# The order of the expert blocks in a two-layer mixture-of-experts trunk: pairs spread evenly, blocks with further rows in every other round

## The chip, the cores and the metric

The kernel runs on one core of one Trainium2 chip. The metric is the device time of one execution in microseconds (us), the median of several runs. TensorE (PE) does the matmuls, VectorE (DVE) and ScalarE (ACT) work element by element, GpSimd (POOL) gathers and scatters rows by index, SyncE (SP) issues the loads of weights from HBM.

## The reference

A trunk of two layers on 1024 frames of 1024 features in fp32. Each layer is a mixer followed by a hierarchical mixture of experts; only the latter is touched:

```python
MOE_EXPERTS = 32; MOE_TOPK = 2; MOE_HIDDEN = 512      # 4 groups of 8 experts
def expert_block(args):
    xb, e = args
    return (jax.nn.silu(xb @ w_gate[e]) * (xb @ w_up[e])) @ w_down[e]
...
out = jnp.zeros((n_tok + 1, d), ys.dtype).at[row_tok].add(ys * row_gate[:, None].astype(ys.dtype))
```

Each frame goes to two of the 32 experts. An expert has gate and up matrices of 1024 x 512 and a down matrix of 512 x 1024, 6 MB in all, so one layer reads 192 MB of expert weights. The order in which experts are worked off doesn't change the result.

## The kernel before

The expert stage of a layer is the function `moe` (L757 to L1016). The experts are ranked by how many frames chose them, and three kinds of blocks follow from the rank:

- a **large block** (`expert`, L861) for each of the 16 experts with most frames (NBIG): 128 rows. Its matmuls are done as three products of split numbers: each half tile of weights is split by ScalarE into whi (L138) and by VectorE into the rest wlo (L139), the rows likewise into xh and xl, and PE adds whi xh, wlo xh and whi xl (`three`, L841);
- the first four of these (NEXT) carry **further rows** too, up to 64 more: they are multiplied with the raw weight tile (L877, L903), which stays occupied until then;
- a **pair** (`pair`, L910) for two of the 16 smaller experts, 64 rows each, side by side in the PE array, with raw weights in fp32 (L919, L928). It needs both experts' weights, 12 tiles of 1 MB, a large block 6.

Inside every block the steps are: a gather of the rows (L790), eight transposes of them (`turn`, into ps_t), gate and up (into ps_g and ps_u), hs = silu(gate) (ACT, L848) times up (DVE, L849), four transposes of hs (into ps_h, L106, called **the turn** below), for a large block its split into hh and hl, down (into ps_y), the evacuation y (DVE, L858) and a scatter (L796). From the last matmul of up to the first of down PE depends on DVE, ACT and its own turn in sequence: **the joint**.

Weight tiles come through a ring: 10 tiles in layer 0, 6 in layer 1. SP issues the loads in the order of the blocks, each when its tile of the ring is free: a large block's tile is free when it is split (or, with further rows, when their matmuls are done), a pair's when PE has read it. The split halves have 7 buffers each for whi and wlo.

The order of the blocks is the list `plan` (L948 to L952): four times a large block with further rows and a pair, then four times three plain large blocks and a pair. The last blocks of the list also decide what `route_over` (L976, the bookkeeping for frames beyond the blocks' rows) stands beside: it is written after the ninth block. Within each engine the instructions stand in a fixed order that a scheduler makes ahead of time from the program; it puts instructions of neighbouring blocks between each other. At run time no engine changes its order.

Of the kernel before, what the change touches and what calls it, by code (L numbers as in the profile page):

```python
# [26 lines left out]
NBIG = 16  # L27
NEXT = 4
# [8 lines left out]
class Core:  # L37
# [725 lines left out]
    def moe(self, o, ctx):  # L763
# [183 lines left out]

        plan, big = [], 0  # L948
        for q in range(NPAIR):
            n = 1 if q < NEXT else 3  # L950
            plan += [("big", b) for b in range(big, big + n)] + [("pair", q)]
            big += n  # L952
        rows = []
        for what, b in plan:
            c = b if what == "big" else NBIG + b
# [1239 lines left out]
```

## Time and profile before

| | |
|---|---|
| median of 3 runs | 3067.4 us (3063.31 to 3076.72) |
| the profiled execution: time, span | 3067.31 us, 3065.6 us |
| mean granted TensorE clock over the span | 0.897 |
| busy over the span: PE, DVE, ACT, POOL | 87%, 58%, 37%, 27% |
| expert stage of layer 0, first to last block | about 824 to 1415 us |
| expert stage of layer 1 | about 2412 to 3005 us |

Busy time of PE is the time with a matmul under way; idle time in a stretch is its length less the busy time. DMA share is the mean busy share of the 16 DMA engines. A wait names the instruction that waited and what released it. In the timeline equal neighbours are merged (x8 means eight), and "idle before" is the engine's own idle time ahead of the row.

### The profile page before, as it was taken

What the parts mean: (1) busy time and instruction counts of PE and PEld (TensorE: products, weight loads), DVE (VectorE), ACT (ScalarE), POOL (GpSimd) and SP (SyncE); (2) the same over time, 40 slices, a digit from 0 to 9 for tenths busy, and PEclk for the clock granted to TensorE, in tenths of its full rate; (3) what the DMA queues carried; (4) which work ended last, traced back from release to release, by engine and by line L of the source; (5) the groups of instructions that cost most, each with busy time, mean ns of one, the idle gap of its engine ahead of it and who ended that gap; (6) DMA issues with size and microseconds to landing.
All of it is one profiled execution on the core that took longest, in us unless ns stands there. A gap on an engine that the chain in (4) does not pass through costs nothing. (4 is left out here: it accounts for less than half of the span.)

```text
span 3065.6 us, 39902 instructions
## 1 busy us (share of the span) xinstructions
PE 2658.0 (87%) x14357; PEld 1855.2 (61%) x14357; DVE 1790.3 (58%) x3207; ACT 1125.4 (37%) x1781; POOL 834.4 (27%) x1161
## 2 busy tenths in 40 slices
PE   4987788989699999995899999999978799998991
PEld 4776456647454466662677777777876444566660
DVE  7546999655633467764734555646557434556674
ACT  4311455432222245552433323323233223345451
POOL 5250665224211031101302533354015111121102
PEclk8898699989799999997898977886988799999996
DMA  8747220223588899997645322243333689999996
GB/s 279 177 125 203 58 59 19 86 69 103 214 336 343 348 368 407 377 388 252 262 132 179 106 73 79 74 115 102 103 124 124 235 343 367 367 363 403 382 385 250
DMA packets 344954, 672.82 MB, mean 219 GB/s; under 512 B 118527, under 2 KB 259871, under 8 KB 293040
## 3 DMA queue, kind: packets, MB, share of 16 engines
q1 hardware_dynamic: 272896, 611.23, 54.5%
q10 hardware_dynamic: 56752, 25.41, 3.1%
q0 software_dynamic: 15104, 33.58, 3.0%
q8 instruction: 115, 1.88, 0.3%
q14 instruction: 87, 0.71, 0.1%
HBM read 611.31 MB, written 79.79 MB: 225 GB/s over the span
## 5 line engine op out<-in xcount | busy, mean ns | idle before, releaser
L139 DVE TENSOR_TENSOR wlo<-w,whi 128x1024 fp32r<-128x1024 f32 x384 | 451.1, 1218 | 112.9 <-ACT whi L138 111.4
L138 ACT ACTIVATE whi<-w 128x1024 fp32r<-128x1024 f32 x384 | 390.3, 1054 | 235.9 <-PE ps_g L841 70.5
L240 PE MATMUL ps_b<-hTh,wh 128*128 128x512 f32 x608 | 260.4, 430 | 26.6 <-ACT cc L1388 12.4
L241 PE MATMUL ps_b<-hTl,wh 128*128 128x512 f32 x608 | 257.0, 423 | 0.0
L790 POOL DMA_INDIRECT xg<-h_d,tok x56 | 80.9, 1445 | 639.6 <-PE ps_t L106 613.1
L242 PE MATMUL ps_b<-hTh,wl 128*128 128x512 f32 x608 | 254.9, 419 | 0.0
L849 DVE TENSOR_TENSOR hs<-hs,ps_u 128x512 f32<-128x512 f32 x48 | 32.9, 685 | 263.3 <-PE ps_u L919 212.4
L796 POOL DMA_INDIRECT ye_d<-y,tab x48 | 71.4, 1487 | 422.3 <-DVE y L858 329.4
L167 DVE SCALAR_TENSOR_TENSOR adacc<-w,cs,adacc 128x256 f32<-128x256 f32 x329 | 162.5, 511 | 5.2
L139 DVE TENSOR_TENSOR wl<-w,wh 128x1024 fp32r<-128x1024 f32 x84 | 104.2, 1255 | 100.8 <-ACT wh L138 100.8
L240 PEld LDWEIGHTS ps_b<-hTh,wh 128*128 128x128 f32 x608 | 125.2, 207 | 54.7 <-ACT cc L1388 13.2
L313 DVE TENSOR_TENSOR_SCAN sP<-keep,sP,sbz 128x256 f32<-128x256 f32 (+1 forms) x160 | 134.8, 885 | 22.7 <-ACT keep L300 10.7
L848 ACT ACTIVATE hs<-ps_g 128x512 f32<-128x512 f32 x48 | 28.7, 598 | 325.0 <-PE ps_g L919 244.7
L919 PE MATMUL ps_g<-w,xh 128*64 128x512 f32 x512 | 143.5, 598 | 0.0
L138 ACT ACTIVATE wh<-w 128x1024 fp32r<-128x1024 f32 x84 | 86.3, 1053 | 154.1 <-PE ps_b L241 135.3
L242 PEld LDWEIGHTS ps_b<-hTh,wl 128*128 128x128 f32 x608 | 124.8, 205 | 28.7 <-issue 0.4
L241 PEld LDWEIGHTS ps_b<-hTl,wh 128*128 128x128 f32 x608 | 125.2, 206 | 27.4 <-issue 0.4
L133 POOL TENSOR_TENSOR rs<-rm,nhalf 128x1 f32<-128x1 f32 (+2 forms) x56 | 48.5, 867 | 330.3 <-DVE rm L131 294.3
L919 PE MATMUL ps_u<-w,xh 128*64 128x512 f32 x512 | 137.6, 595 | 0.0
L315 POOL TENSOR_TENSOR sw<-sw,sP 128x512 f32<-128x512 f32 (+1 forms) x80 | 99.2, 1241 | 135.3 <-DVE sP L313 61.9
L928 PE MATMUL ps_y<-w,hh 128*64 128x512 f32 x512 | 122.0, 598 | 2.2 <-ACT hh L923 2.2
L1705 POOL TENSOR_TENSOR T<-N,X 128x60 f32<-128x60 f32 (+24 forms) x248 | 85.8, 346 | 126.5 <-DMA N<-n_d 108.3
(712 smaller groups left out, 6178.9 us busy)
## 6 DMA issues: line engine op xcount, KB each, us to landing
w<-in_moe_w_gate_dram SPq DMA_DIRECT2D x128, 1024.0 KB, 14.6
w<-in_moe_w_up_dram SPq DMA_DIRECT2D x128, 1024.0 KB, 14.6
w<-in_moe_w_down_dram SPq DMA_DIRECT2D x128, 1024.0 KB, 13.4
w<-in_ada_w_dram SPq DMA_DIRECT2D x48, 1024.0 KB, 6.0
w<-in_odd_w_in_dram SPq DMA_DIRECT2D x26, 1024.0 KB, 5.6
cy<-ye_d SPq DMA_DIRECT2D x16, 1024.0 KB, 14.5
cx<-xm_d SPq DMA_DIRECT2D x21, 512.0 KB, 7.2
w<-in_even_w_in_dram SPq DMA_DIRECT2D x8, 1024.0 KB, 8.6
```

What stands on the lines that cost most here:

```text
L138: self.nc.scalar.activation(hi, x, AF.Copy)
L139: self.nc.vector.tensor_tensor(lo, x, hi.bitcast(FT), op=OP.subtract)
L167: eng.scalar_tensor_tensor(acc, wk, ck, acc, op0=OP.mult, op1=OP.add)
L240: nc.tensor.matmul(p, a[0], b[0], start=first, stop=False)
L241: nc.tensor.matmul(p, a[0], b[1], start=False, stop=False)
L242: nc.tensor.matmul(p, a[1], b[0], start=False, stop=last)
L313: v.tensor_tensor_scan(P[:, r, 0:n][:, ::-1], keep[:, r, 0:n][:, ::-1], zero.to_broadcast([128, n]), P[:, r, n:n + 1], op0=OP.mult, op1=OP ...
L315: g.tensor_tensor(w[:, :, 0:n], w[:, :, 0:n], P[:, :, 1:n + 1], op=OP.mult)
L790: nc.gpsimd.indirect_dma_start(out=xg, out_offset=None, in_=h_d[:], in_offset=bass.IndirectOffsetOnAxis(ap=tokc, axis=0), bounds_check=T - ...
L919: nc.tensor.matmul(ps[z][r], x[:, 4 * h + k, r], w[z][h][:, k, :], start=(h == 0 and k == 0), stop=(h == 1 and k == 3))
L928: nc.tensor.matmul(py[n][r], ht[:, f, r], w[2][f // 2][:, f % 2, two[n]], start=(f == 0), stop=(f == 3))
L1705: g.tensor_tensor(o, N[:, 0:j, j:j + 1].to_broadcast([128, j, w]), X[:, j:j + 1, c:8].to_broadcast([128, j, w]), op=OP.mult)
```

## The change

```diff
--- before.py
+++ after.py
@@ -947,9 +947,9 @@
 
         plan, big = [], 0
         for q in range(NPAIR):
-            n = 1 if q < NEXT else 3
-            plan += [("big", b) for b in range(big, big + n)] + [("pair", q)]
-            big += n
+            n = q // 2 if q % 2 == 0 else NEXT + big
+            big += q % 2
+            plan += [("big", n), ("pair", q), ("big", NBIG - 1 - q)]
         rows = []
         for what, b in plan:
             c = b if what == "big" else NBIG + b
```

NPAIR is 8, NBIG 16, NEXT 4. Before, the plan is, with the number of each large block: 0, pair, 1, pair, 2, pair, 3, pair, 4, 5, 6, pair, 7, 8, 9, pair, 10, 11, 12, pair, 13, 14, 15, pair. After: 0, pair, 15, 4, pair, 14, 1, pair, 13, 5, pair, 12, 2, pair, 11, 6, pair, 10, 3, pair, 9, 7, pair, 8: eight rounds of a large block, a pair and a plain large block. Blocks 0 to 3, those with further rows, open the first, third, fifth and seventh round. The same blocks run, with the same weights; the order of gathers, loads and scatters follows the plan, and so does the scheduler's order on every engine.

On PE, layer 0, the joint of the tenth large block of the plan before (the last plain one before a pair). ps_u, ps_g and ps_y are written by gate, up and down; L919 is the pair that follows:

```order
L841 MATMUL ps_u<-whi,xl 128x512
L106 MATMUL ps_h<-ident,hs 128x128 x4
L919 MATMUL ps_g<-w,xh 64x512
L106 MATMUL ps_t<-ident,xg_6647 128x128 x8
L919 MATMUL ps_g<-w,xh 64x512 x7
L919 MATMUL ps_u<-w,xh 64x512 x8
L919 MATMUL ps_g<-w,xh 64x512 x8
L841 MATMUL ps_y<-whi,hh 128x512
L841 MATMUL ps_y<-wlo,hh 128x512
L841 MATMUL ps_y<-whi,hl 128x512
```

After, PE, layer 0, the joint of the plain large block that closes the fourth round (number 12):

```order
L841 MATMUL ps_u<-whi,xl 128x512
L106 MATMUL ps_t<-ident,xg_6643 128x128 x8
L106 MATMUL ps_h<-ident,hs 128x128 x4
L841 MATMUL ps_y<-whi,hh 128x512
L841 MATMUL ps_y<-wlo,hh 128x512
L841 MATMUL ps_y<-whi,hh 128x512
L841 MATMUL ps_y<-wlo,hh 128x512
L841 MATMUL ps_y<-whi,hl 128x512 x2
```

Before, 24 matmuls of the pair stand between the turn and down; after, down follows the turn directly, and only the next block's transposes stand ahead of the turn.

On DVE, layer 0, from hs of the sixth pair of the plan before; the first two evacuations y are those of the large block ahead of it, the other two its own; xl and wlo are splits of rows and weights of what follows:

```order
L849 TENSOR_TENSOR hs<-hs,ps_u 128x512
L139 TENSOR_TENSOR xl<-ps_t,xh 128x512 x2
L139 TENSOR_TENSOR wlo<-w,whi 128x1024 x3
L858 TENSOR_TENSOR y<-ps_y,g2row 128x512 x2
L139 TENSOR_TENSOR wlo<-w,whi 128x1024 x8
L858 TENSOR_TENSOR y<-ps_y,g2row 128x512 x2
L139 TENSOR_TENSOR wlo<-w,whi 128x1024
L849 TENSOR_TENSOR hs<-hs,ps_u 128x512
L139 TENSOR_TENSOR wlo<-w,whi 128x1024 x2
L139 TENSOR_TENSOR xl<-ps_t,xh 128x512 x2
```

After, from hs of the sixth round's pair; again the first two evacuations are those of the large block ahead of it and the last two its own:

```order
L849 TENSOR_TENSOR hs<-hs,ps_u 128x512
L139 TENSOR_TENSOR xl<-ps_t,xh 128x512 x2
L858 TENSOR_TENSOR y<-ps_y,g2row 128x512 x2
L139 TENSOR_TENSOR wlo<-w,whi 128x1024 x9
L825 COPY xh<-ps_t 128x512
L139 TENSOR_TENSOR wlo<-w,whi 128x1024
L849 TENSOR_TENSOR hs<-hs,ps_u 128x512
L139 TENSOR_TENSOR wlo<-w,whi 128x1024 x2
L139 TENSOR_TENSOR hl<-ps_h,hh 128x512
L858 TENSOR_TENSOR y<-ps_y,g2row 128x512 x2
```

Before, the pair's evacuations stand ahead of the next large block's hs; after, they stand behind that block's hl.

## Rows read from the trace of the kernel before

**Rows 1.** Stretches of the expert stages: busy us and (x) instructions by engine, clock, DMA
```profile
core 0: us, PE busy (x) PEld busy (x) DVE busy (x) ACT busy (x) POOL busy (x), PEclk, DMA share, GB/s
824.00:1072.70 248.70, 243.56 (x1051) 120.12 (x1051) 90.90 (x136) 70.71 (x89) 25.37 (x24) 1.00 0.85 340
1072.70:1415.00 342.30, 323.06 (x1426) 213.59 (x1425) 221.81 (x239) 170.88 (x196) 55.69 (x28) 1.00 0.92 372
2412.60:2660.60 248.00, 244.02 (x1047) 121.77 (x1045) 90.55 (x132) 74.28 (x93) 26.58 (x25) 0.99 0.84 337
2660.60:3005.00 344.40, 324.20 (x1432) 214.35 (x1431) 221.90 (x242) 167.69 (x193) 46.78 (x27) 1.00 0.96 384
2930.10:3005.00 74.90, 72.87 (x319) 46.53 (x317) 42.02 (x45) 32.38 (x37) 4.64 (x4) 1.00 0.98 404
```

**Rows 2.** What PE waited for, 1072.7 to 1415 us: total, times, longest
```profile
PE ps_h L106 <- DVE hs L849: 8.5, 9, 1.6
...
PE ps_g L841 <- DVE wlo L139: 3.1, 4, 1.2
...
PE ps_g L841 <- ACT whi L138: 2.4, 3, 1.6
...
PE ps_u L841 <- DVE wlo L139: 0.9, 2, 0.7
```

**Rows 3.** The same of 2660.6 to 3005 us
```profile
PE ps_h L106 <- DVE hs L849: 8.7, 7, 2.5
...
PE ps_y L841 <- DVE y L858: 2.7, 1, 2.7
...
PE ps_g L841 <- DVE wlo L139: 1.8, 3, 0.8
...
PE ps_g L841 <- ACT whi L138: 1.6, 2, 1.2
...
PE ps_u L841 <- DVE wlo L139: 0.3, 1, 0.3
```

**Rows 4.** Timeline of PE: start, us, instruction, in brackets idle before and releaser
```profile
1088.09 1.04 PE L106 MATMUL ps_h<-ident,hs 128*128 128x128 f32 x4 [1.60 <-DVE hs L849]
...
1108.50 1.23 PE L106 MATMUL ps_t<-ident,xg 128*128 128x128 f32 x8 [0.46 <-ACT xh L823]
...
1111.84 0.49 PE L841 MATMUL ps_g<-whi,xh 128*128 128x512 f32 x1 [1.63 <-ACT whi L138]
...
1175.99 0.75 PE L106 MATMUL ps_h<-ident,hs 128*128 128x128 f32 x4 [0.85 <-DVE hs L849]
...
1407.63 2.80 PE L928 MATMUL ps_y<-w,hh 128*64 128x512 f32 x12 [0.69 <-ACT hh L923]
...
2676.63 0.74 PE L106 MATMUL ps_h<-ident,hs 128*128 128x128 f32 x4 [2.50 <-DVE hs L849]
...
2680.87 0.50 PE L841 MATMUL ps_y<-whi,hl 128*128 128x512 f32 x1 [1.07 <-DVE hl L139]
...
2764.23 0.74 PE L106 MATMUL ps_h<-ident,hs 128*128 128x128 f32 x4 [1.84 <-DVE hs L849]
...
2768.98 0.47 PE L841 MATMUL ps_y<-whi,hh 128*128 128x512 f32 x1 [2.75 <-DVE y L858]
2769.29 0.39 PE L841 MATMUL ps_y<-wlo,hh 128*128 128x512 f32 x1
2769.52 0.40 PE L841 MATMUL ps_y<-whi,hl 128*128 128x512 f32 x1
```

**Rows 5.** What the load queue (SP) waited for, 824 to 1072.7, then 1072.7 to 1415
```profile
SPq L943 <- PE ps_e L903: 61.6, 8, 17.6
...
SPq L943 <- PE ps_e L877: 54.4, 10, 14.9
...
SPq L943 <- DVE wlo L139: 111.5, 49, 6.4
```

**Rows 6.** Timeline of PE: the last pair of layer 1, its down matmuls
```profile
2999.68 4.89 PE L928 MATMUL ps_y<-w,hh 128*64 128x512 f32 x22
```

## The prediction

> **What bounds the kernel now.** I read the page's 40 slices first: between 800 and 1420 us and between 2410 and 3010 us, the expert stages of the two layers, TensorE (PE), the DMA share and the TensorE clock are all near their tops at once. The diff touches these two stages alone, some 1190 of 3065.6 us. Then I cut each stage where the order of blocks changes: a first stretch in which large blocks with further rows and pairs alternate (four of each), and a second with three plain large blocks to each pair (twelve and four). In the first, PE is busy 243.56 of 248.70 us and 244.02 of 248.00, with a DMA share of 0.85 and 0.84; in the second 323.06 of 342.30 and 324.20 of 344.40, with 0.92 and 0.96 [rows 1]. So the first stretch is PE's: its idle time is 5.1 and 4.0 us, 1.8%. The second is nearly DMA's as well, and PE idles 19.2 and 20.2 us there, 5.7%. The clock is granted in full, 0.99 to 1.00. Nothing that PE does is removed by the change: before and after, each layer has the same matmuls on it. **The gain therefore has a hard end**: if every idle microsecond of both stages went, 5.1 + 4.0 + 19.2 + 20.2 = 48.5 us would be won.
>
> What is that idle time? The waits of PE in the second stretch name it. The transposes of the hidden rows (L106 into ps_h) wait for the product hs: 8.5 and 8.7 us. The matmuls that wait for split weights (whi, wlo), so for weights that came late, make 3.1 + 2.4 + 0.9 = 6.4 us in layer 0 and 1.8 + 1.6 + 0.3 = 3.7 us in layer 1 [rows 2, 3]. The first kind isn't supply: it is the joint inside a large block, where gate and up are done, ScalarE and VectorE form hs, PE turns it, both engines split it, and only then down can start. PE is in order, so a joint costs what the order puts into it. A joint with seven matmuls of the next large block inside idles 0.85 us. A bare one, with no expert matmul between the turn and down, idles 1.60 us; 2.50 + 1.07 = 3.57; 1.84 + 2.75 = 4.59; and, with the next block's eight transposes ahead of the turn, 0.46 + 1.63 = 2.09 [rows 4].
>
> **The change, part by part.** The sum starts at the profiled execution, 3067.31 us (its span of 3065.6 and 1.7 around it), beside the median of 3067.4.
>
> Supply. Before, the second stretch asks for 30 weight tiles per 85.6 us (342.3 over four groups) and the first for 18 per 62.2 us (248.7 over 4). After, every round of large block, pair, plain block asks for 24. Rounds with further rows are longer on PE than on DMA, so the loads, which in the first stretch wait for tiles that the further rows hold (61.6 + 54.4 us, against 111.5 us for splits in the second) [rows 5], get time to run ahead; plain rounds eat that lead. I count all 10.1 us of late weights as gone, less the 1.63 that I price in the joints: **-8.5 us**. Its ends are 0 and -10.1.
>
> Joints. The program orders each engine ahead of time, and this is what the diff doesn't show. I counted for the 24 plain large blocks of both layers whether at most one expert matmul stands between the turn and down. Before, 4 are bare (the four above): 1 with the transposes ahead of the turn, 3 without. After, 20 are: 12 with, 8 without; blocks that overlapped now stand one behind the other. That adds 11 of the one kind and 5 of the other. A bare joint costs more than a filled one by 2.09 - 0.85 = 1.24 us in the first kind, and by the mean of 1.60, 3.57 and 4.59, 3.25, less 0.85 = 2.40 in the second [rows 4]: 11 x 1.24 + 5 x 2.40 = **+25.6 us**. Nothing covers it: PE is the engine whose end sets the stage. For the low end the 12 lose only the 0.46 of the transposes and the 0.69 that a pair waits for its hh [rows 4], 0.30 over a filled joint, and the 5 lose 1.60 - 0.85 = 0.75: 3.3 + 3.8 = 7 us. For the high end all 16 cost 4.59 - 0.85 = 3.74: 60 us. I take the middle because the rows are of the same two kinds; the low end has a point in its favour, since after, down often begins with the four matmuls that read hh before the first that reads hl.
>
> VectorE's order. In layer 0's sixth round the pair's evacuations now stand behind hl of the plain block that follows, whose down matmuls need the pair's two banks; before, the sixth pair's stood ahead of the next block's hs. The 2.75 us wait for an evacuation in layer 1 [rows 3, 4] is such a case, and one of the four bare joints. Not counted again.
>
> The rest. The further rows' matmuls are the same and are cut into as many pieces within a handful: 0. The bookkeeping of the overflow (L976) still falls beside a block with further rows and the plain one behind it: 0. The order of the mixer between the two stages shifts a little too, with the same instructions: 0, and 6 us either way, a guess. The stage ends on a plain block instead of a pair: its bare joint is counted.
>
> Sum: 3067.3 - 8.5 + 25.6 = **3084 us**, 0.55% slower. About 0.5% (15 us) is what a measurement of this kernel can tell from no change.
>
> **Rivals.** (A) *Faster, 3040 us.* The change evens out the demand, and PE idles everywhere as it does in the first stretch, 1.8%. Then the second stretches' 39.4 us of idle time become 686.7 x 0.018 = 12.6, and 26.8 us are won. For it: the two stretches have different scarce resources [rows 1]. Against it: most of the idle time named in rows 2 and 3 is joints, and the order after makes them bare; it decides once a bare joint costs no more than a filled one. The Trainium skill, page "Perfetto Trace Analysis", section "Optimization Strategy", says that where the most-contended engine changes between regimes, interleaving the regimes may help. By that rule the outcome is this rival. The trace agrees that there are two regimes (DMA share 0.85 against 0.92, 0.84 against 0.96), but it also shows the second with PE busy at 94%, so that little is left to mix. The same page of the Trainium skill, section "Identifying the Most-Contended Engine", warns that matmul busy time is no measure of headroom; here the starts 0.23 us apart in a full run [rows 4] are what I rest on, and the pace that stands in them can't be changed by an order.
>
> (B) *No difference, 3066 us.* Supply as above and joints at their low end: 3067.3 - 8.5 + 7. For it: the four hh matmuls ahead, and idle times that overlap with late weights. It is also what comes out if both resources are so full that any order gives the same pace.
>
> (C) *Slower still, 3106 us.* The plain rounds run out of weights. A pair's PE time is 96 x 4.89/22 = 21.3 us [rows 6] and 2.1 of transposes; a plain large block's is then (323.06 - 4 x 23.4)/12 = 19.1. A plain round needs 2 x 19.1 + 23.4 + joints of some 6 = 68 us of PE. Its 24 tiles of 1.05 MB and its gathers and scatters, about 3 MB, take 28.3/0.384 = 74 us at the second stretch's rate in layer 1 [rows 1]. It is 6 us short unless the round before ran ahead, and the ring of weight tiles is 6 deep in layer 1 (10 in layer 0). If the lead fails in layer 1, four rounds lose 22 us; in both layers 44, 3128. Against it: the rate reached 404 GB/s in the last group [rows 1], and rounds with further rows have some 10 us to spare.
>
> **How the numbers follow.** Forecast 0.40, A 0.12, B 0.34, C 0.14. The range leaves out A and the upper half of C, and takes in B with the mixer's 6 us and late weights at their end: 3058 to 3112. Faster by over 0.5% is A, 0.12. The same is B, 0.34. Slower is the forecast and C, 0.54.
>
> **What would show it.** Right: PE's idle time within each expert stage rises from 24 us to some 33; its waits for hs, hh and hl grow, and those for whi and wlo shrink; the DMA share is even at about 0.9. A: idle time falls to 15 us a stage. B: it stays at 24, with other names. C: waits for whi and wlo grow in the plain rounds, and with them a DMA share near 1 there. I am wrong at the root if the busy time itself changes, by the clock or by matmuls that run at another pace, or if the difference lies outside the two stages.

## The result

The changed kernel takes 3133.91 us (median of 4 runs, 3130.29 to 3154.07) beside 3069.68 for the kernel before (4 runs, 3063.31 to 3076.72): 1.0229 times as long, 95% interval 1.0209 to 1.025. It is slower, as forecast, but by 64 us and not by 17, and 3133.91 lies above the range (3058 to 3112).

Where the 64 us lie is read by cutting both traces into the first expert stage, the mixer between the stages, and the second expert stage. First the kernel before, then the changed one; the columns are those of [rows 1].

```profile
core 0: us, PE busy (x) PEld busy (x) DVE busy (x) ACT busy (x) POOL busy (x), PEclk, DMA share, GB/s
823.70:1415.10 591.40, 566.92 (x2476) 334.01 (x2475) 313.11 (x374) 241.71 (x285) 81.05 (x52) 1.00 0.89 359
1415.10:2412.70 997.60, 862.69 (x5859) 690.61 (x5859) 549.41 (x1126) 330.89 (x660) 319.42 (x605) 0.83 0.42 131
2412.70:3005.00 592.30, 568.13 (x2476) 336.09 (x2475) 312.40 (x374) 241.96 (x285) 73.37 (x52) 0.99 0.91 365
```

```profile
821.80:1437.40 615.60, 582.16 (x2476) 335.50 (x2475) 312.76 (x374) 241.03 (x285) 75.68 (x52) 0.98 0.86 344
1437.40:2448.20 1010.80, 863.63 (x5858) 690.15 (x5858) 542.97 (x1125) 330.67 (x660) 310.01 (x605) 0.83 0.42 129
2448.20:3069.30 621.10, 586.73 (x2477) 343.86 (x2475) 313.20 (x374) 240.20 (x285) 76.93 (x52) 0.97 0.87 348
```

The stages grew by 24.2 and 28.8 us, the mixer by 13.2, and what comes before is 1.9 shorter: 64.3. In each stage, take busy from length: PE's idle time went from 24.5 to 33.4 us and from 24.2 to 34.4, together +19.2. **But its busy time rose as well**, by 15.2 and 18.6 us, with the same matmuls. The DMA share fell. The mixer has nearly the same busy time as before (862.69, 863.63); 12 of its 13 us are idle time.

What PE waited for in the changed kernel, layer 0 and then layer 1 (total us, times, longest); [rows 2, 3] answer to them for the second stretches:

```profile
PE ps_h L106 <- DVE hs L849: 11.7, 12, 2.0
PE ps_y L841 <- ACT hh L138: 4.7, 9, 0.7
PE ps_y L841 <- DVE hl L139: 4.1, 6, 1.2
PE ps_y L841 <- DVE y L858: 3.9, 2, 2.8
PE ps_g L841 <- DVE wlo L139: 2.8, 4, 1.5
...
PE ps_u L841 <- DVE wlo L139: 1.0, 1, 1.0
```

```profile
PE ps_h L106 <- DVE hs L849: 11.9, 13, 1.8
PE ps_g L841 <- DVE wlo L139: 5.3, 6, 1.5
PE ps_y L841 <- ACT hh L138: 3.4, 6, 0.7
PE ps_y L841 <- DVE y L858: 3.2, 2, 2.1
...
PE ps_y L841 <- DVE hl L139: 2.3, 6, 1.0
...
PE ps_g L841 <- ACT whi L138: 1.4, 2, 1.2
```

The joint's waits (hs, hh, hl and y, a pair's 0.7 for hh in each layer with them) make 25.1 and 21.5 us, where the same rows of the kernel before make 11.0 and 13.9: +21.7. Late weights (whi, wlo) make 3.8 and 6.7 us instead of 7.7 and 5.0: -2.2. So the added idle time is the joints', as the prediction said. The kernel before, its whole stage of layer 0:

```profile
PE ps_h L106 <- DVE hs L849: 9.6, 11, 1.6
PE ps_g L841 <- DVE wlo L139: 4.4, 6, 1.2
...
PE ps_g L841 <- ACT whi L138: 2.4, 3, 1.6
```

One bare joint in TensorE's timeline of the changed kernel, with the next block's transposes ahead of the turn:

```profile
1277.77 1.23 PE L106 MATMUL ps_t<-ident,xg 128*128 128x128 f32 x8 [0.46 <-ACT xh L823]
1279.76 0.75 PE L106 MATMUL ps_h<-ident,hs 128*128 128x128 f32 x4 [0.76 <-DVE hs L849]
1283.32 0.47 PE L841 MATMUL ps_y<-whi,hh 128*128 128x512 f32 x1 [2.81 <-DVE y L858]
...
1283.86 0.43 PE L841 MATMUL ps_y<-whi,hl 128*128 128x512 f32 x1
1284.10 0.62 PE L841 MATMUL ps_y<-whi,hh 128*128 128x512 f32 x1
1284.52 0.63 PE L841 MATMUL ps_y<-wlo,hh 128*128 128x512 f32 x1
```

```profile
1278.00:1284.00 6.00, 2.43 (x15) 1.99 (x15) 6.00 (x8) 5.05 (x6) 2.15 (x2) 1.00 1.01 421
1284.00:1287.50 3.50, 3.50 (x10) 2.67 (x9) 3.18 (x3) 0.00 (x0) 0.00 (x0) 0.51 1.03 421
```

Idle 0.46, 0.76 and 2.81 us, with VectorE busy throughout (6.00 of 6.00). And **then the clock falls**: the granted clock is 1.00 up to 1284 and 0.51 behind it, which is the 1.2 GHz level, and the matmuls start 0.42 us apart instead of 0.23. By the trace's record of the clock, it stood at that level for 22.0 and 33.9 us of the two stages, in the kernel before for 5.2 and 10.3. At half pace, half of these 40.4 us more would be lost, 20 us. The starts of all matmuls in the two traces give the split of the 33.8 us by which busy time rose, each matmul counted up to the start of the next and compared with the mean of its line in unbroken runs at the full clock, in the kernel before: 21.8 us are in matmuls at the lower level, 6.6 in those just ahead of and just behind a gap, 4.6 where one kind of matmul follows another, 0.8 in all others. At the edge of a gap a matmul adds more because in a run it shows 0.39 us of busy time and adds 0.23, while the last one before a gap adds all of it and the first behind adds 0.31.

The Trainium skill, page "TensorE: Matmul & The Clock Gate", section "Part 1: The HAM clock gate (the "warmup" mystery)", says that the array is at its lower clock by default and that activity releases it. The rows above agree: the clock falls behind 6 us of which PE was busy for 2.43. The last section shows a fall that busy time alone does not explain.

### The profile page after: what moved, and what is told of

Read it like the earlier page. It is cut to its first block, busy times and chain, and to the rows that moved or that the text cites. A ratio compares the mean times of both kernels' runs of the same rounds, so it can differ in the third digit from the quotient of the medians.

```text
span 3129.6 us, 39865 instructions
## 1 busy us (share of the span) xinstructions
PE 2689.2 (86%) x14357; PEld 1860.8 (59%) x14357; DVE 1783.7 (57%) x3207; ACT 1122.5 (36%) x1781; POOL 827.0 (26%) x1161
## 5 line engine op out<-in xcount | busy, mean ns | idle before, releaser
L919 PE MATMUL ps_u<-w,xh 128*64 128x512 f32 x512 | 140.6, 595 | 0.0
L241 PEld LDWEIGHTS ps_b<-hTl,wh 128*128 128x128 f32 x608 | 122.9, 202 | 27.8 <-issue 0.8
L919 PE MATMUL ps_g<-w,xh 128*64 128x512 f32 x512 | 139.0, 597 | 0.0
L928 PE MATMUL ps_y<-w,hh 128*64 128x512 f32 x512 | 137.5, 613 | 1.4 <-ACT hh L923 1.4
L841 PE MATMUL ps_y<-whi,hh 128*128 128x512 f32 x256 | 107.5, 422 | 15.2 <-ACT hh L138 8.1
```

What stands on the lines that cost most here:

```text
L241: nc.tensor.matmul(p, a[0], b[1], start=False, stop=False)
L841: nc.tensor.matmul(p, x[a][:, k, :], w(b, j)[:, ns], start=(first and a + b == 0), stop=(last and a == 1))
L919: nc.tensor.matmul(ps[z][r], x[:, 4 * h + k, r], w[z][h][:, k, :], start=(h == 0 and k == 0), stop=(h == 1 and k == 3))
L928: nc.tensor.matmul(py[n][r], ht[:, f, r], w[2][f // 2][:, f % 2, two[n]], start=(f == 0), stop=(f == 3))
```

## Experiments

In them J is the theory of the prediction, with the clock added: bare joints cost idle time, and the clock falls in them. S is rival C: weights come late in the new order. H came up on the way: blocks with further rows hold their weight tiles too long, so the loads stop. "Bare" counts all joints with at most one expert matmul between the turn and down, now of pairs and of blocks with further rows too (these have a second turn; the last one counts): **10 and 9 before, 22 and 16 after**, in layers 0 and 1.

### One layer at a time (l0new, l1new)

```diff
+        if i == 0:
             plan, big = [], 0
             for q in range(NPAIR):
                 n = q // 2 if q % 2 == 0 else NEXT + big
...
+        else:
+            plan, big = [], 0
+            for q in range(NPAIR):
+                n = 1 if q < NEXT else 3
...
```

(l1new has `if i == 1`.)

> The new order of blocks in layer 0 only; layer 1 keeps the old one. The rows of the changed kernel lay 24.2 us in layer 0's expert stage, 13.3 us in the mixer behind it, 28.6 us in layer 1's expert stage. Theory J (bare joints on TensorE's queue, idle time and a clock that falls in them): the pieces add, since each stage carries its own bare joints. Layer 0's stage about 615 us (before 591.3), layer 1's about 592 as before; the mixer, whose instructions stand on TensorE in exactly the order of the changed kernel here, about 1011 (before 997.6). Time 3105 us, ratio 1.0115. Theory S (supply: weights that come late in rounds without further rows, worst in layer 1, whose ring of tiles is the smaller): layer 0 gives less than half, under 1.010. If the mixer's 13 us were chance and not its order: ratio about 1.007.

> The new order of blocks in layer 1 only. The mixer stands on TensorE in exactly the order of the kernel before. Theory J: layer 0's stage 591, mixer 998, layer 1's stage about 621 (before 592.4): time 3098 us, ratio 1.0093. If the mixer's 13 us came from anything but its order, the mixer is near 1011 here. Theory S: layer 1 is the place where weights run out, ratio over 1.010 and the waits for split weights (whi, wlo) over 15 us, against 6.7 in the changed kernel.

Measured: l0new 1.0154 (1.0123 to 1.0184), l1new 1.0096 (1.0074 to 1.0117). The first stage and the mixer of l0new, then the mixer and the second stage of l1new; their other stages took 592.7 and 595.2 us:

```profile
823.80:1439.50 615.70, 582.34 (x2476) 335.36 (x2475) 312.95 (x374) 240.83 (x285) 72.50 (x52) 0.98 0.86 344
1439.50:2456.40 1016.90, 872.76 (x5858) 697.50 (x5858) 546.17 (x1126) 330.79 (x660) 311.40 (x605) 0.82 0.42 129
```

```profile
1423.10:2423.50 1000.40, 859.43 (x5859) 688.21 (x5859) 549.19 (x1126) 330.71 (x660) 318.29 (x605) 0.83 0.43 131
2423.50:3036.30 612.80, 579.04 (x2476) 337.03 (x2475) 312.81 (x374) 240.45 (x285) 76.53 (x52) 0.99 0.87 352
```

The pieces add (1.54% and 0.96% beside 2.29%), and each stage is slow only where its blocks are new. S fails in both: l0new is over its 1.010, l1new under it, with 5.2 us of waits for weights where S asked for over 15. J's 1.0115 for l0new is missed by a mixer of 1017 us. **The mixer's loss goes with the mixer's own order**: 1011 and 1017 us in the two kernels that have the new one, 998 and 1000 where it is the old one (and 995 and 996 in before_pin2 and before_ring, which have the old one too). Its size isn't firm, though: after_hi and after_hi_pin2 below have one order there on every engine and mixers of 1011 and 1027 us, at a granted clock of 0.83 and 0.81. Layer 1 came out 8 us better than in the changed kernel with PE in the same order: the clock was at its lower level for 12.8 us here and for 33.9 there, and PE was busy 7.7 us less. So 8 of that stage's 29 us are not fixed by the order.

### Joints filled by hand (after_pin, before_pin, after_pin2, before_pin2)

```diff
-                expert(xg, ws[0], ...)
+                g = expert(xg, ws[0], ...)
...
+            m = next(g)
+            if behind is not None:
+                with tc.issue_after(getattr(m, "ins", m)):
+                    for _ in behind:
+                        pass
+            next(g)
+            behind = g
```

`expert` and `pair` stop once after their first 12 or 8 matmuls and once ahead of down; down of the block before is then queued on PE behind these matmuls. The pin2 kernels do so behind large blocks alone.

> The changed kernel's blocks in the changed kernel's order, but TensorE's order within them is set by hand: each block's down matmuls are queued behind the first 12 gate and up matmuls of the next large block, or the first 8 gate matmuls of the next pair (issue order alone, no data). That leaves 4 bare joints of 24 in each layer, where the changed kernel has 22 and 16 (large blocks and pairs together). Same instructions, same loads, but each block's first weights are needed a down phase (some 11 us) earlier. Theory J: the waits for hh and hl (8.8 and 5.7 us in the stages of the changed kernel) go, TensorE's idle time falls from 34 to about 22 us a stage, and the half-clock time in the stages (22 and 34 us) falls under 10 each, so its busy time returns to 567 to 572 us: stages about 592 to 596 us each, time about 3070 to 3085 us with a mixer that may be ordered in its own way (plus or minus 13). Theory S: weights are late, so asking for them sooner only turns the waits for hh and hl into waits for whi and wlo; stages stay at 612 us or over, time 3125 or over. A rival of the clock's part: if half clock comes from the mixture of pair and large matmuls and not from the joints, idle falls but busy time stays at 582 and 587: stages about 605, time about 3110.

> The kernel before with the same hand-set order: 4 bare joints of 24 in each layer, where the kernel before has 10 and 9. Theory J: idle time falls from 24 to about 15 us a stage, half-clock time is small already (5.2 and 10.3 us); stages about 582, time 3050 us give or take 13 for the mixer's order. Theory S: in the second stretch, where the DMA share is 0.92 and 0.96, weights needed 11 us sooner are late instead: waits for whi and wlo grow by what the joints give back, time 3070 or over.

> The changed kernel with the hand-set order behind large blocks alone: a large block's down matmuls are queued behind the next large block's first 12 gate and up matmuls, or the next pair's first 8. Behind a pair the order is left to the program, since after_pin showed that the block behind a pair has no weights yet (TensorE stood 3 to 8 us for whi there, and the clock fell with it). Bare joints left: 3 and 4 large ones of 16 (changed kernel 14 and 9), all 8 pairs. Theory J (idle time in bare joints, and a clock that falls in them): waits for hh and hl go, idle time about 26 us a stage (changed kernel 33.5 and 34.6), half-clock time under 15 us a stage (22 and 34), stages about 600 us each: time 3090 to 3105 us with a mixer 998 to 1017, ratio 1.007 to 1.013. Theory S (weights are late at every joint of this order): stages as in after_pin, 625 us and over, ratio 1.03. Between them, joints filled but the clock as low as before: stages about 608.

> The kernel before with the hand-set order behind large blocks alone. Bare joints: 4 and 3 large ones as before, now other ones, and 8 pairs a layer instead of 6, while many of the filled ones hold 17 to 19 matmuls instead of 7. The mixer stands on TensorE in exactly the order of the kernel before. Theory J: within 10 us of the kernel before, stages 586 to 596 us, ratio 0.995 to 1.003. Theory S: the second stretch with its DMA share of 0.92 and 0.96 has no weights to give earlier; the joint between two plain large blocks then stalls for whi, stages over 600, ratio over 1.006.

Measured: after_pin 1.0307 (1.0286 to 1.0328), before_pin 1.0204 (1.0177 to 1.0231), after_pin2 1.0247 (1.0218 to 1.0275), before_pin2 1.0041 (1.0024 to 1.0057). The stages were 627 and 632, 616 and 619, 616 and 616, 597 and 599 us. J's numbers fail in all four, in the last narrowly (597 and 599 us instead of 586 to 596, 1.0041 instead of at most 1.003); S's 600 us and 1.006 are not reached there either. PE's waits in layer 0 of after_pin, then of after_pin2:

```profile
PE ps_g L841 <- ACT whi L138: 22.3, 6, 7.9
...
PE ps_g L841 <- DVE wlo L139: 4.8, 9, 1.0
```

```profile
PE ps_g L841 <- DVE wlo L139: 13.9, 13, 1.5
...
PE ps_g L841 <- ACT whi L138: 6.8, 7, 1.8
```

The waits for hh and hl are gone (0.7 us left), and **waits for weights stand in their place**: 27.8 us (0.7 of them into ps_u) and 20.7 us for whi and wlo where the changed kernel has 3.8. With this order of blocks, what the joints are filled with isn't ready yet. What a missing weight looks like, behind a pair of after_pin:

```profile
1194.63 1.34 PE L106 MATMUL ps_t<-ident,xg 128*128 128x128 f32 x8
1203.92 0.80 PE L841 MATMUL ps_g<-whi,xh 128*128 128x512 f32 x1 [7.95 <-ACT whi L138]
```

```profile
1193.00:1196.00 3.00, 2.13 (x14) 1.67 (x12) 1.89 (x3) 1.69 (x3) 0.00 (x0) 1.00 0.99 407
1196.00:1204.00 8.00, 0.08 (x1) 0.08 (x1) 0.10 (x1) 1.19 (x2) 0.95 (x1) 0.73 1.01 426
1204.00:1208.00 4.00, 3.54 (x8) 2.46 (x9) 3.86 (x4) 3.03 (x4) 0.00 (x0) 0.50 1.01 426
```

The DMA engines are busy throughout (a share of 1.01, at 426 GB/s), so these weights are late because their loads started late. The clock falls during the stall and stays at 0.50 behind it. So S is right about these kernels; of the changed kernel, which asks for the same weights a joint and a down later, it explains nothing, since late weights cost it no more than before.

### The two halves of the change (spread_first, alt_groups)

```diff
+        plan = [("big", 0), ("pair", 0), ("big", 15), ("big", 1), ("pair", 1), ("big", 14), ("big", 2), ...
```

```diff
+        plan = [("big", 0), ("pair", 0), ("big", 4), ("big", 5), ("big", 6), ("pair", 1), ("big", 1), ...
```

> Half of the change: eight rounds of large block, pair, plain block as in the changed kernel, but the four blocks with further rows stand in the first four rounds and not in every other one. Here the program leaves fewer joints bare: 6 and 6 large, 7 and 7 pairs (changed kernel 14 and 9, 8 and 7; kernel before 4 and 3, 6 and 6). Theory J: 3 more bare joints in each layer than before at 2 to 4 us with the clock: stages 597 to 603 us, ratio 1.004 to 1.012 with a mixer of 998 to 1017. Theory S: four plain rounds in a row (large, pair, plain) run out of weights, and worse than the changed kernel: ratio 1.02 or over, with the waits for whi and wlo over 15 us a stage. If it is the even spread of the pairs itself that costs (a pair for every two large blocks), it is as slow as the changed kernel: stages 612 or over.

> The other half of the change: the blocks with further rows go in every other round, but the plain ones keep their rows of three: further, pair, three plain, pair, four times. The program leaves 12 and 10 joints bare, large and pairs together (kernel before 10 and 9, changed kernel 22 and 16). Theory J: hardly slower than before, stages 593 to 599 us, ratio 1.002 to 1.009 with a mixer of 998 to 1017. Theory S: three plain blocks in a row stand behind only one block with further rows, so a lead of loads is short: like before's second stretch, ratio 1.00. If the spread of the further rows itself costs, stages 605 or over.

The 12 and 10 in the second text count large blocks alone; with pairs it is 20 and 18, for which 2 us a joint would give 611 and 610 us. From here on a stage goes from its first matmul to its last, 0.3 to 0.4 us less than the stretches above, unless its stretch is shown. Measured: spread_first 1.0117 (1.0098 to 1.0135), stages 598.1 and 606.8; alt_groups 1.0129 (1.0112 to 1.0147), stages 600.6 and 599.9, mixer 1017. Each half costs 7 to 15 us a stage and both together 24 and 29, so neither is it alone. Spread_first fits J in its ratio and in layer 0, while layer 1's 606.8 lies above J's 603. Alt_groups lies just above J's recorded 599 us and, with half of its loss in the mixer, above J's 1.009; its stages are 10 us below what its bare joints would cost at 2 us. S's 1.02 and 1.00 did not come.

### Tiles held, split halves (after_ring, before_ring, after_hi, before_hi)

```diff
-        hl = own.enter_context(tc.tile_pool(name=f"hl{i}", bufs=7))
+        hl = own.enter_context(tc.tile_pool(name=f"hl{i}", bufs=5))
...
-            keep.enter_context(self.ring("d0", 4))
+            keep.enter_context(self.ring("d0", 6))
```

(In the ring kernels `e1`, layer 1's part of the ring, goes from 5 to 7 too. The hi kernels' down, not shown, changes like the gate and up here.)

```diff
-                            nc.tensor.matmul(p, xe[:, 4 * h + k, :], ws[z][h][:, k, :], start=first, stop=last)
+                            nc.tensor.matmul(p, xe[:, 4 * h + k, :], w[z](0, k).bitcast(FT), start=first, stop=last)
```

H rests on the load queue's waits for the further rows in the changed kernel (layer 0; [rows 5] answer to them), and on stretches like the second one here, with 26 GB/s between two busy ones:

```profile
SPq L943 <- PE ps_e L877: 69.8, 8, 16.0
SPq L943 <- PE ps_e L903: 59.1, 8, 16.5
```

```profile
1000.00:1006.00 6.00, 5.66 (x27) 2.50 (x25) 4.80 (x27) 0.60 (x1) 0.00 (x0) 1.00 0.84 330
1006.00:1014.00 8.00, 8.00 (x39) 4.95 (x39) 4.13 (x8) 0.39 (x1) 1.01 (x1) 1.00 0.07 26
1014.00:1020.00 6.00, 6.00 (x32) 2.89 (x30) 0.82 (x3) 0.00 (x0) 0.00 (x0) 1.00 1.00 349
```

> The changed kernel with two more weight tiles in the ring of each layer (12 and 8, before 10 and 6), paid for by five buffers for each kind of split half (before seven). Theory H (holes in the loads, formed from the traces so far): the six tiles of a block with further rows are held until the further rows' matmuls are done, the ring is full, and the loads stand still; the time without data adds up to 82 and 65 us a stage in the kernel before and 95 and 85 us in the changed kernel, while the time with data stays near 510 to 535 us in every kernel. Two more tiles let some 5 us more of data pass in each of a stage's 8 or so holes: holes 30 us a stage shorter, stages about 585 to 595 us, time about 3065 to 3090, ratio 1.00 to 1.008. Theory J (bare joints): the program leaves 5 and 7 joints bare here (changed kernel 22 and 16), so it expects much the same in this kernel; the two differ in before_ring. If the split buffers are what counts, slower than the changed kernel: ratio over 1.025.

> The kernel before with the same two more weight tiles and two fewer buffers for each kind of split half. The mixer stands on TensorE in the order of the kernel before; 10 joints are bare in each layer (kernel before 10 and 9). Theory H: the four holes of 10 us behind the blocks with further rows shrink by some 5 us each, and others with them: stages 565 to 580 us (before 591), time 3020 to 3045 us, ratio 0.985 to 0.993. Theory J: no gain, ratio 0.997 to 1.003. If the split buffers count more than the tiles: ratio over 1.005.

> The changed kernel, but the further rows multiply with the high half of the split weights in place of the raw tile; their precision is lower by that, the number of matmuls is the same. The raw tile of a block with further rows is then free as soon as it is split, as a plain block's is. Bare joints: 15 in each layer (changed kernel 22 and 16). Theory H: the queue's waits for the further rows' matmuls (70 and 59 us in layer 0 of the changed kernel) go, the holes behind these blocks with them; time without data falls from 95 and 85 us to 60 or less, stages about 585 to 592 us: time 3065 to 3090, ratio 1.00 to 1.008. Theory J: a third of the bare joints goes in layer 0 and none in layer 1: stages about 606 and 620, ratio 1.018 or over.

> The kernel before with the further rows on the high half of the split weights in the same way; lower precision of these rows, same number of matmuls. Bare joints: 9 and 7 (kernel before 10 and 9). Theory H: the four holes of 10 us behind the blocks with further rows go, the second stretch starts with loads ahead: stages 565 to 580 us, ratio 0.985 to 0.993, give or take 0.004 for the mixer's order; the distance to after_hi is under 15 us a stage. Theory J: stages 587 to 591, ratio 0.997 to 1.003; the distance to after_hi is 15 us and over.

Measured: after_ring 1.0537 (1.051 to 1.0564), before_ring 1.0272 (1.0254 to 1.0289), a miss for both theories: five split buffers, or the order that the program makes with them, lose far more than two tiles could win (layer 0 of after_ring: 36 us of waits for whi and wlo, granted clock 0.93). After_hi 1.0112 (1.0094 to 1.0131), stages 599.2 and 599.7, 16 and 21 us under the changed kernel; before_hi 1.0016 (1.0002 to 1.0031), stages 598 and 590. After_hi lies between H's 592 and J's 606; before_hi wins nothing, against H, and layer 0's 598 is above J's 591; the distance to after_hi, 1 and 9 us, is under the 15 that J asked for. So letting go of the tiles sooner gains time in the new order and none in the old one. It isn't the tiles alone: PE's order changes with it.

### Both at once, and a milder form (after_hi_pin2, after_efirst, before_efirst)

```diff
+                for k in range(4 if more is not None else 0):
+                    for z, p in enumerate(quad):
+                        nc.tensor.matmul(p, xe[:, 4 * h + k, :], ws[z][h][:, k, :], ...)
                 w = [halves(ws[z][h]) for z in range(2)]
```

(This is the efirst kernels'; the same matmuls no longer stand between the three-part ones. After_hi_pin2 joins the diffs of after_hi and after_pin2.)

> The changed kernel with the further rows on the high half of the split weights (lower precision of these rows, tiles free once they are split) and the joints behind large blocks filled by the hand-set order of after_pin2. Bare joints 8 and 7, where after_hi has 15 and 15; its stages were 599.2 and 599.7 us. The mixer stands on TensorE in the order of after_hi. Theory H (held tiles, loads that stand still, late weights) with joints as the second cause: once the weights are there a filled joint pays, stages 585 to 592 us, time 3070 to 3090, ratio 1.000 to 1.006. Theory H alone, joints only a place where late weights are waited for: stages within 4 us of after_hi, ratio 1.010 to 1.013. If filling asks for weights that still are late, as in after_pin2: stages 605 or over.

> The changed kernel; in a block with further rows the gate and up matmuls of the further rows for one half of the weights are written ahead of that half's three-part matmuls and not between them, so they read the raw tile as it arrives and let go of it sooner. Same arithmetic. The down tiles are held as before. Bare joints 18 in each layer (changed kernel 22 and 16). Theory H: the queue's waits for these matmuls (70 and 71 us a stage) shrink by half or more, time without data from 95 and 85 us to about 80 and 70, stages 600 to 608 us: ratio 1.011 to 1.017. Theory J (bare joints): layer 0 4 joints better, layer 1 2 worse, stages about 610 and 620, ratio about 1.021.

> The kernel before with the same earlier place of the further rows' gate and up matmuls; same arithmetic. Bare joints 10 and 13 (kernel before 10 and 9). Theory H: the holes behind the four blocks with further rows are shorter, but they lie beside blocks that keep TensorE busy anyway (before_hi gained nothing there): stages 583 to 592 us, ratio 0.993 to 1.003, with a mixer of 995 to 1011. Theory J: layer 1 slower by 4 more bare joints, stage 600 or over.

Measured: after_hi_pin2 1.0184 (1.0159 to 1.0209), stages 607; after_efirst 1.0142 (1.0121 to 1.0163), stages 609 and 616; before_efirst 1.0092 (1.0071 to 1.0113), stages 591 and 597.5, over half of its loss a mixer of 1010. Filling by hand loses 8 us a stage even with the tiles free, against both forms of H: PE waits 21.6 us in layer 0 for whi and wlo, 5.0 in after_hi. After_hi_pin2 loses twice as much, 16 us, in the mixer, where its order is after_hi's. In after_efirst and before_efirst, letting go of the gate and up tiles sooner gains 6 and 4.5 us in the new order and nothing in the old one.

### Bare joints under the old order (before_hl8, before_hl6, after_hl6)

```diff
-        hl = own.enter_context(tc.tile_pool(name=f"hl{i}", bufs=7))
+        hl = own.enter_context(tc.tile_pool(name=f"hl{i}", bufs=8 - i))
...
-            keep.enter_context(self.ring("d0", 4))
+            keep.enter_context(self.ring("d0", 3))
```

(The hl6 kernels have `bufs=6` and the ring as it was.)

> The kernel before; in layer 0 one more buffer for each kind of split half (8) and one tile fewer in the ring (9). The program then leaves 14 large and 8 pair joints bare in layer 0, as many as in the changed kernel (14 and 8; kernel before 4 and 6), with the old order of blocks. Layer 1 has the sizes of before and 12 bare joints (before 9). Theory J (a bare joint costs by itself): layer 0's stage 610 to 620 us, as in the changed kernel. Theory H (late weights by the order of the blocks): layer 0's stage 588 to 600 us. Layer 1: 592 to 600. The mixer stands in another order: 998 to 1017.

> The kernel before with six buffers for each kind of split half in place of seven, nothing else. Bare joints 12 in each layer (10 and 9). If split halves are scarce: half of what two fewer cost in before_ring (46 and 38 us), so stages 605 to 620 us, ratio 1.008 to 1.020. If they aren't, and before_ring lost for its other order: stages 588 to 598, ratio 0.998 to 1.006.

> The changed kernel with six buffers for each kind of split half in place of seven, nothing else. Bare joints 22 and 16 and the mixer's order are those of the changed kernel. If split halves are scarce in its order too: stages 625 to 640 us, ratio 1.03 to 1.04. If bare joints and late tiles are what limits it, with halves to spare: stages 613 to 623, ratio 1.020 to 1.026.

Measured: before_hl8 1.0129 (1.0108 to 1.015), before_hl6 1.0038 (1.0023 to 1.0053), after_hl6 1.0219 (1.0202 to 1.0236), all beside 3083.06 us for the kernel before on that chip, 0.4% more than elsewhere, so some 2 us of a stage are the chip's. Layer 0 of before_hl8 and its waits:

```profile
834.80:1447.40 612.60, 579.03 (x2476) 338.95 (x2475) 310.20 (x373) 237.84 (x284) 91.91 (x52) 0.98 0.87 346
```

```profile
PE ps_h L106 <- DVE hs L849: 14.2, 13, 1.9
PE ps_g L841 <- DVE wlo L139: 7.7, 8, 1.5
PE ps_y L841 <- ACT hh L138: 4.2, 8, 0.7
...
PE ps_y L841 <- DVE hl L139: 1.1, 2, 0.9
```

**This is the clearest run.** The blocks stand in the old order, late weights cost what they cost before (7.7 us in both), but 22 joints are bare, and the stage takes 612.6 us, as J said and not H: idle 33.6, busy 579.0, clock 0.98, each nearly the changed kernel's 33.4, 582.2 and 0.98. One tile fewer in the ring isn't likely to be the reason by itself: in the kernel before, layer 1 runs with six tiles in the same time as layer 0 with ten. The load queue does wait longer for tiles that are being split (168.4 us instead of 115.6), but PE's waits for weights show nothing of it. After_hl6 stays at 614.7 and 620.3: halves are to spare at six, so the 40 us of the ring kernels come between six and five, or from their other order; that wasn't tried apart.

Over the 26 stages of the 13 kernels whose order the program made (without the ring kernels), stage time goes with the bare joints of large blocks at 2.1 us for each (587 us at none), correlation 0.80, with a scatter of 6 us. That is a fit and no test; the rows are a choice:

```
kernel, layer      bare (large)  stage us  us at the lower clock
before 0             10 (4)       591.1      5.2
before 1              9 (3)       591.9     10.3
spread_first 1       13 (6)       606.8     20.3
after_hi 0           15 (8)       599.2     11.3
alt_groups 0         20 (12)      600.6     14.9
after_efirst 1       18 (11)      616.2     25.4
before_hl8 0         22 (14)      612.3     20.7
after 0              22 (14)      615.2     22.0
after 1              16 (9)       620.7     33.9
```

The time at the lower clock itself goes with the bare joints only loosely (correlation 0.5): before_hi stood at that level for 23.8 and 18.2 us with 9 and 7 bare joints, the kernel before for 5.2 and 10.3 us with 10 and 9.

No version beat the kernel before.

## Why the prediction was wrong in size

- **The whole.** The sum put +17.1 us on the stages' idle time and nothing elsewhere. Idle time rose by 19.2. What is missing is 33.8 us of busy time and 13.2 us of the mixer.
- **The bound.** "PE is the engine whose end sets the stage": nothing here speaks against it. The DMA share fell, and VectorE and ScalarE were busy in each stage for what they were before, to 2 us.
- **Supply, -8.5.** Wrong: late weights fell by 2.2 us, from 12.7 to 10.5. They fell in layer 0 and rose in layer 1. The loads did not run ahead in the rounds with further rows; they stood still there, at 26 GB/s, and the queue's waits for tiles that further rows held were 128.9 us in layer 0, beside 116.0 before [rows 5].
- **Joints, +25.6.** The mechanism was right, and the joint's waits grew by 21.7 us. The price of the first kind came out by luck: it is one row's 2.09 us, of which 1.63 are a wait for whi, so supply [rows 4], and the changed kernel's 12 such joints idle 2.1 us each. The 8 of the second kind idle 1.8 us each instead of 3.25. PE's idle time in a stage was named as rising "from 24 us to some 33"; it rose to 33.4 and 34.4, with hs, hh and hl as named; that the total fits so well is luck in part, since supply gave 6 us less and joints cost less than priced. But the term counted idle time alone, and only plain large blocks. With the blocks with further rows and the pairs, 19 more joints are bare, not 16, and a bare joint can also cost busy time, by the clock and at the edges of its gaps. Layer 0 of before_hl8 shows the whole price: some 19 us of the stage for 10 large and 2 pair joints more, of which idle time is 9.1.
- **Busy time, counted as unchanged.** This is the step that failed first, and the prediction named it as its root risk: "if the busy time itself changes, by the clock". It rose by 33.8 us, 21.8 of them in matmuls at the lower clock. The clock's "0.99 to 1.00" before was read as a given, and "the pace that stands in them can't be changed by an order" was said of the matmuls' starts; behind the joint shown above they stand 0.42 us apart instead of 0.23. In before_hl8 the clock fell to 0.98 with more bare joints and no new order of blocks.
- **The mixer, "0, and 6 us either way, a guess".** It cost 13.2 us, 12.3 of them idle time. l0new against l1new shows that a loss goes with the new order of the same instructions; how much of the 13.2 is the order is open, since one order can come out 16 us apart, and which instructions of it was not looked for.
- **The rivals.** A (interleaving) and B are out: idle time rose and the stages are longer. C is half right in another way than worked out: the new order leaves loads late in the sense that nothing is there to fill a joint with (after_pin, after_pin2), and held tiles may have a part (after_hi), but the waits for weights did not grow. C's 3106 to 3128 came nearest in time, by a mechanism that the changed kernel's waits don't show.

Left open: how far the bare joints of the changed kernel, and how far the late loads behind them, would be curable alone. Filling joints needs weights sooner, and freeing tiles (after_hi) also changes the order on PE and so the joints; no run separated the two in layer 1, where 6 more bare large joints came with 29 us and the fitted price explains 13. There after_hi, with 15 bare joints instead of 16, is 21 us faster, which the number of bare joints does not explain.

## What to carry to other kernels

Before counting an order's idle time, look at what else a gap breaks: new gaps can cost busy time too, through the clock and at their edges, here 33.8 us beside 19.2 of idle time. A static order that leaves a gap bare may do so because nothing is ready; see whether the data would be there before filling it by hand. And a change of order in one stage can reorder another: compare that stage's order too, and give it a price from both sides.

## What the hardware showed

The clock fell without a long stall. Here a pair's joint in the changed kernel, idle for 0.85 us and then filled with transposes, and the granted clock beside it:

```profile
935.45 4.02 PE L919 MATMUL ps_u<-w,xh 128*64 128x512 f32 x15
940.32 0.75 PE L106 MATMUL ps_h<-ident,hs 128*128 128x128 f32 x4 [0.85 <-DVE hs L849]
940.99 1.85 PE L106 MATMUL ps_t<-ident,xg 64*128 64x64 f32 x12
```

```profile
936.00:942.60 6.60, 5.75 (x32) 2.96 (x28) 1.89 (x3) 2.68 (x5) 0.16 (x1) 1.00 1.01 426
942.60:946.20 3.60, 3.60 (x7) 0.80 (x5) 0.00 (x0) 0.93 (x2) 0.85 (x1) 0.53 1.01 428
946.20:950.00 3.80, 3.80 (x19) 1.81 (x20) 0.00 (x0) 2.87 (x4) 0.99 (x1) 1.00 1.02 426
```

PE is busy for 5.75 of the 6.60 us ahead, yet the clock is at 0.53 right behind. What stood just before it fell were 16 transposes: a joint filled with transposes looks full by its busy time, and the clock fell all the same. In this layer it fell at the three pair joints where 12 or 16 transposes of the next block follow the turn, and at none of the five with 8 or fewer; in layer 1 one with 12 went by without a fall.
